# Sliding-window copy: which direct copies go whole and which in two halves

## The chip, the cores and the metric

The kernel runs on one core of a Trainium2 chip. The metric is device time in microseconds (us), the median of several runs. The kernel does no arithmetic: everything that takes time is a transfer by the core's 16 DMA engines.

## The reference

```
x: (32, 4096, 256) float32, window_size = 64, stride = 32
n_windows = (4096 - 64) // 32 + 1          # 127
for i in range(n_windows):
    result[:, i] = x[:, 32 * i : 32 * i + 64]
```

Call 32 rows of x (32 x 256 float32, 32 KB) a block. A batch of x has 128 blocks, and window i of a batch is block i followed by block i + 1. So nearly every block is written twice: as the first half of its own window and as the second half of the window before. The output is 266 MB, the input 134 MB.

## The kernel before

**Two ways for the data.** Batches 1, 4, 7, ..., 31 (11 of 32) are *staged*: `Staging.load` brings the 128 blocks of a batch (4 MB) into one of six SBUF tiles `xb`, one block to a partition, and `Staging.store` writes the tile out twice, once as first halves and once as second halves of windows (4 MB each). The other 21 batches go *directly* from DRAM to DRAM, by `Copier.windows`.

**The staging ring** is issued on ScalarE's DMA queue (`ring_s`, q10 in the profile): six loads, six items' stores, five loads, five items' stores. The descriptors are 16 KB, so a load or one half of an item's store gives each of the 16 engines 16 data packets and one semaphore packet: 17 packets. Of the first and last items some transfers are cut smaller. A store also writes one half-window that belongs to the neighbour batch, which is why the windows at the batch edges are written later.

**The direct copies** are issued on SyncE's DMA queue (`ring_d`, q1). `sixteens` lists 147 groups of 16 windows (1 MB of output each). A group goes in one of two forms:

- *whole*: one DMA of 16 rows of 64 KB; each engine gets two 32 KB packets and one semaphore packet, 3 packets ("turns" in the code);
- *halves*: one DMA with the 16 first halves and one with the 16 second halves, 512 KB each; each engine gets two times one 32 KB packet and one semaphore packet, 4 packets.

Both forms move the same bytes. The loop at L175 chooses by an accumulator, `share`, that grows per group; when it reaches 120, 120 is taken off and the group goes in halves. `turns` counts the packets that one engine has got from this queue, and the ring's own packets are taken to pass at the same count: `first_loads` = 102, then 204 for the stores, `loads` = 85. `loading` (L178) is true in the two loading stretches so counted. Neither the order of the groups nor anything on the ring's queue depends on the form chosen.

**The end.** The DMA before the last group's signals `near` (L176). GpSimd's queue (`ring_r`, q0) waits for it (L192) and then issues the 21 `edges`, up to 15 windows each (20.5 MB with the columns of L200), waiting for the store of each neighbouring staged item (L196). SyncE waits for the last item's first stores (L201) and then copies two last windows in columns (L202). The kernel ends when all counts are in (L204).

Of the kernel before, what the change touches and what calls it, by code (L numbers as in the profile page):

```python
# [125 lines left out]
@with_exitstack  # L126
def kernel(
    ctx: ExitStack,
    tc: tile.TileContext,
    x: bass.AP,  # L130
    window_size: bass.AP,
    stride: bass.AP,
    out: bass.AP,
):
    nc = tc.nc
    W, S = int(window_size), int(stride)
    B, L, D = x.shape
    n_win = (L - W) // S + 1
    assert out.shape == (B, n_win, W, D)
    c = Copier(x, out, B, L, D, W, S, n_win)  # L140


    staged = [*range(1, B, 3)]
    items = [(b, -1 if b == B - 1 else 0, c.nb) for b in staged]
    place = {b: g for g, (b, _, n) in enumerate(items) if n == c.nb}
    direct = [b for b in range(B) if b not in staged]
    pool = ctx.enter_context(tc.tile_pool(name="xb", bufs=1))
    st = Staging(c, tc, pool, x.dtype, items, 6)
    ring_d, ring_s, ring_r = nc.sync, nc.scalar, nc.gpsimd
    done = tc.alloc_semaphore("done")  # L150
    near = tc.alloc_semaphore("near")
    rest = tc.alloc_semaphore("rest")
    total = {done: 0, near: 0, rest: 0}

    def count(dma, sem):
        dma.then_inc(sem, 16)
        total[sem] += 16

    sixteens = []
    for b in direct:
        w = 15 if b - 1 in staged else 0
        sixteens += [(b, w + 16 * j) for j in range((c.nw - w) // 16)]
    singles = [(B - 1, c.nw - 1, 1)]
    edges = [(b, 0 if b - 1 in staged else 112, 15) for b in direct[:-1]]
    last = B - 2
    edges.append((last, 112, 4))

    first_loads, loads, stores = 6 * 17, 5 * 17, 6 * 34  # L170
    turns = share = 0
    with tc.tile_critical():  # L172
        st.run(ring_s)

        for i, (b, w) in enumerate(sixteens):  # L175
            sem = near if i == len(sixteens) - 2 else done  # L176
            second = turns - first_loads - stores
            loading = turns < first_loads or 0 <= second < loads  # L178
            share += 120 if turns < 16 or -8 <= second < 16 else 90 if loading else 18
            if share >= 120:  # L180
                share -= 120
                turns += 4
                count(c.windows(ring_d, b, w, 16, 0), done)
                count(c.windows(ring_d, b, w, 16, 1), sem)
            else:
                turns += 3
                count(c.windows(ring_d, b, w, 16), sem)
            if i == len(sixteens) // 2:
                for b, w, half in singles:
                    count(c.windows(ring_d, b, w, 1, half, 2048), done)  # L190

        ring_r.wait_ge(near, 16)  # L192
        for b, w, n in edges:
            for k in (b - 1, b + 1):
                if k in place and b != last:
                    st.wait_stored(ring_r, place[k])  # L196
            count(c.windows(ring_r, b, w, n), rest)


        count(c.columns(ring_r, last, 116, 9), rest)  # L200
        st.wait_stored(ring_d, place[B - 1])  # L201
        count(c.columns(ring_d, last, 125, 2), done)  # L202
        total[st.ended] = st.count[st.ended]
        for sem, n in total.items():  # L204
            ring_d.wait_ge(sem, n)
# [35 lines left out]
```

## Time and profile before

| | |
|---|---|
| time, median of 3 runs | 744.95 us (744.84 to 745.9) |
| span of the profiled execution | 749.4 us |
| profiled execution's own time | not recorded apart from its span |
| mean rate of the 16 DMA engines over the span | 418 GB/s |
| bytes moved by DMA | 313.26 MB in 18290 packets |
| GpSimd issues the first 18 edges | 654.4 to 664.7 us |
| the other 3 and the columns | 702.0 to 704.3 us |
| SyncE issues the last columns | 729.8 us, landing after 9.4 us |

A packet is one descriptor's worth of data on one DMA engine (here 16 KB or 32 KB, and a few bytes for a semaphore). The windows view of the profile gives, for each stretch, the busy time and count of the compute engines (here GpSimd alone, which only issues), the granted TensorE clock (no matter here), the DMA engines' mean busy share and the GB/s that they moved.

### The profile page before, as it was taken

The page shows a single profiled execution, that of the slowest core. Times are in us where ns is not written, and L with a number is a line of the kernel's source. Part 1 is how long each engine was busy: PE and PEld are TensorE (multiplying, and loading weights), DVE is VectorE, ACT ScalarE, POOL GpSimd, SP SyncE. Part 2 cuts the span into 40 slices and gives each one's busy share as a digit, 9 for nine tenths or more (in the row PEclk, how much of TensorE's full clock was granted, in tenths as well). Part 3 has the DMA queues.
Part 4 walks back from the last instruction along what each step waited for, and adds up shares of the span by engine and source line. Part 5 has one row for each costly group of instructions (what it writes and reads, how often), then busy time and mean ns, then how long its engine had stood idle before and what let it go on. Part 6 is the DMA issues. An engine that isn't in the chain of part 4 may idle for free.

```text
span 749.4 us, 322 instructions
## 1 busy us (share of the span) xinstructions
POOL 12.8 (2%) x26
## 2 busy tenths in 40 slices
POOL 0000000000000000000000000000000000040100
DMA  8999999999999999999999999999999999999996
GB/s 360 401 427 429 427 429 428 434 423 418 420 424 423 418 424 415 422 427 427 414 427 417 429 432 429 430 422 430 429 423 421 423 421 419 425 426 423 431 409 262
DMA packets 18290, 313.26 MB, mean 418 GB/s; under 512 B 4336, under 2 KB 4336, under 8 KB 4528
## 3 DMA queue, kind: packets, MB, share of 16 engines
q1 hardware_dynamic: 8016, 154.32, 48.8%
q10 hardware_dynamic: 9104, 138.41, 44.0%
q0 software_dynamic: 1168, 20.51, 6.5%
q14 instruction: 2, 0.02, 0.0%
HBM read 220.95 MB, written 267.09 MB: 651 GB/s over the span
## 4 chain that ended last, share of the span: by engine, by line
another core or an unknown queue 92%; POOL 2%; issue 0%; POOLq 0%; SPq 0%
POOL out_dram L34 2%; POOL out_dram L44 0%; POOLq L236 0%; SPq L172 0%; POOLq L114 0%
## 5 line engine op out<-in xcount | busy, mean ns | idle before, releaser
L34 POOL DMA_DIRECT2D out_dram<-in_x_dram x21 | 12.0, 576 | 691.3 <-DMA out_dram<-in_x_dram 654.0
L44 POOL DMA_DIRECT2D out_dram<-in_x_dram x1 | 0.6, 581 | 0.0
L222 POOL MEMSET const-float32-0.0<- 128x1 f32 x1 | 0.1, 98 | 0.2 <-issue 0.2
L222 POOL MEMSET const-bfloat16-1.0<- 128x1 bf16 x1 | 0.1, 101 | 0.0
L222 POOL MEMSET const-float32-1.0<- 128x1 f32 x1 | 0.1, 98 | 0.0
L222 POOL MEMSET const-uint8-127<- 128x1 uint8 x1 | 0.1, 98 | 0.0
## 6 DMA issues: line engine op xcount, KB each, us to landing
out_dram<-in_x_dram SPq DMA_DIRECT2D x92, 1024.0 KB, 100.7
out_dram<-xb ACTq DMA_DIRECT2D x21, 4096.0 KB, 139.7
out_dram<-in_x_dram SPq DMA_DIRECT2D x110, 512.0 KB, 90.3
xb<-in_x_dram ACTq DMA_DIRECT2D x10, 4096.0 KB, 131.4
out_dram<-in_x_dram POOLq DMA_DIRECT2D x20, 960.0 KB, 38.5
xb<-in_x_dram ACTq DMA_DIRECT2D x4, 1024.0 KB, 15.7
out_dram<-xb ACTq DMA_DIRECT2D x2, 1024.0 KB, 113.4
out_dram<-xb ACTq DMA_DIRECT2D x4, 512.0 KB, 96.9
```

Of the source, the lines that this page charges most:

```text
L34: return q.dma_start(out=self.oap((b * self.nw + w0) * 2 + h, [[2 * blk, n], row]), in_=self.xap(b * self.nb + w0 + h, [[blk, n], row]), m ...
L44: return q.dma_start(out=self.oap((b * self.nw + w0) * 2, [[part, 16], [2 * self.blk, n], row]), in_=self.xap(b * self.nb + w0, [[part, 16 ...
L222: nc = _bacc.Bacc("TRN2", target_bir_lowering=False, num_devices=1)
```

## The change

The step of `share` is replaced. Before, groups go in halves in the first 16 turns and from 8 turns before the second loads to 16 turns into them, three in four while the ring loads, and 18 in 120 while it stores. After, they go in halves in the first 16 turns, whole while the ring loads, and 82 in 120 while it stores.

```diff
             loading = turns < first_loads or 0 <= second < loads
-            share += 120 if turns < 16 or -8 <= second < 16 else 90 if loading else 18
+            share += 120 if turns < 16 else 0 if loading else 82
             if share >= 120:
```

Counted by running the loop, by the stretch in which `turns` stands when a group is issued:

| stretch | before: halves / whole | after: halves / whole |
|---|---|---|
| first loads | 21 / 6 | 4 / 29 |
| first stores | 11 / 54 | 38 / 18 |
| second loads | 18 / 4 | 0 / 28 |
| second stores | 5 / 28 | 20 / 10 |
| all | 55 / 92 (496 turns) | 62 / 85 (503 turns) |

The order within the stores is, after, halves, halves, whole, repeated, with three halves in a row now and then. The instructions of ScalarE's and GpSimd's queues are unchanged; SyncE's queue has seven instructions more.

## The prediction

> **What bounds the kernel now.** I read the page first. Three DMA queues carry everything, and together they fill the 16 engines' time.
>
> ```profile
> q1 hardware_dynamic: 8016, 154.32, 48.8%
> q10 hardware_dynamic: 9104, 138.41, 44.0%
> q0 software_dynamic: 1168, 20.51, 6.5%
> HBM read 220.95 MB, written 267.09 MB: 651 GB/s over the span
> ```
>
> The three shares make 99.3% of the span: the engines have no idle time to win back, and the change moves no byte (a group is 1 MB in either form). Time can only come from the pace of the packets, so next I cut the span into stages in the windows view. The cuts are where the ring's packet count (the DMA view of a window from 0: 1680 packets of q10 by 131.7 us, 105 per engine) shows loads turning into stores.
>
> ```profile
> 0.00:35.00 35.00, 0.20 (x4) 1.00 0.94 377
> 35.00:131.00 96.00, 0.00 (x0) 1.00 1.01 428
> 131.00:150.00 19.00, 0.00 (x0) 1.00 1.01 434
> 150.00:405.00 255.00, 0.00 (x0) 1.00 1.00 422
> 405.00:412.00 7.00, 0.00 (x0) 1.00 1.02 405
> 412.00:513.00 101.00, 0.00 (x0) 1.00 1.01 429
> 513.00:530.00 17.00, 0.00 (x0) 1.00 1.00 431
> 530.00:650.00 120.00, 0.00 (x0) 1.00 1.01 422
> ```
>
> The last column is GB/s. The loading stages, mostly halves, run at 428 and 429. The storing stages, mostly whole, run at 422, except for their first 17 to 19 us (434, 431). An undisturbed pace is about 431: the packet records have medians of 1213 ns for 32 KB, 611 ns for 16 KB and 9 ns for a semaphore, and a whole group beside three ring packets comes to 430 by these, a pair of halves beside four to 429, plus under 1% because packets overlap by some 4 ns. So form alone makes no pace: the loss is in packets that last longer than their median. Summed over the records it is 15.0 us per engine. Storing at 422 instead of 431 for 255 and 120 us is 7.8 us of it, loading 1.1 us; the rest is the start and the end.
>
> The two queues alternate packet by packet: by 654 us q1 had 7949 packets and q10 7954. That lets me place each group in time: its turn number times 16 is its place among q1's packets. Of the storing stages, three stretches of halves, two of halves where one store DMA ends and the next begins, and three of whole groups:
>
> ```profile
> 205.30:210.20 4.90, 0.00 (x0) 1.00 1.01 431
> 262.00:266.80 4.80, 0.00 (x0) 1.00 1.01 434
> 349.70:354.60 4.90, 0.00 (x0) 1.00 1.00 428
> 292.60:296.90 4.30, 0.00 (x0) 1.00 1.00 412
> 318.20:323.00 4.80, 0.00 (x0) 1.00 0.97 410
> 157.80:175.30 17.50, 0.00 (x0) 1.00 1.00 419
> 275.10:288.20 13.10, 0.00 (x0) 1.00 1.00 420
> 569.30:577.90 8.60, 0.00 (x0) 1.00 1.00 419
> ```
>
> And single whole groups amid the loads:
>
> ```profile
> 96.30:100.50 4.20, 0.00 (x0) 1.00 1.03 437
> 114.50:118.80 4.30, 0.00 (x0) 1.00 1.03 442
> 476.70:480.90 4.20, 0.00 (x0) 1.00 1.00 429
> ```
>
> In a storing stage halves run undisturbed in mid-store and slow at a store's end; whole groups are slow throughout. Amid loads a whole group is not slow. Windows this short carry packets over their edges, so I take prices from the records: the time above the median, as a share of all packet time while a group passes. Storing: 81 whole groups 2.30%, 14 pairs of halves 0.99% (the pair at 406 us, where stores turn into loads, apart: 10.3%). Loading, from 36 us on: 9 whole groups 0.60%, 33 pairs 0.77%.
>
> **Part by part. Storing.** A whole group takes 3 turns and about 4.2 us, a pair 4 turns and 4.86 us. Before, whole groups fill 82 x 4.2 = 344 us of the stores' 422 us, 81%; after, 28 x 4.2 = 118 us beside 58 x 4.86 = 282 us, 29%. So 52% of 400 us goes from 2.30% to 0.99%: 400 x 0.52 x 1.31% = 2.7 us won. Bounds: by the windows view alone (13 stretches of halves average 424.1 GB/s, the stage 422, so whole ones 421.5) the difference is 0.6% and the gain 1.3 us; if halves free the stores down to the loading stages' 0.74%, it is 2.16% less 0.74% of 400 us, 5.7 us. The row nearest to the changed code is the 14 pairs, so 2.7.
>
> **Loading.** 34 pairs fewer, 47 whole groups more; the stages last longer for the direct stream moves more per turn, but this is shifted work, not added work. From 36 us on some 230 us change form. By the nine whole groups the price is 0.60% less 0.77%, nothing; by the storing rows it would be 2.30% less 0.74%, 3.6 us lost. I take 0, because those nine ran in this very stage; but none of them ran beside another whole group, so the other bound stays in the range.
>
> **The start.** Up to 35 us the rate is 377. Turns under 16 stay halves, the fifth group stays whole (12.1% above the median at 22 to 26 us), but the sixth and seventh (8.7% and 1.5%, 5 us each) become whole. At the fifth's 12.1% that is 5 x 3.4% and 5 x 10.6%, 0.7 us lost; at the price of later whole groups it is a gain of 0.5. I take 0.3 lost, nearer to the loss since the fifth is their neighbour.
>
> **The turn into the second loads.** The halves laid around it go: at 405 to 412 us the rate was 405 in spite of them. Nothing in the trace shows what whole groups do there; at 2.3% instead of 10.3% they would win 0.4 us, at a doubled price lose 0.5. I take 0.
>
> **Semaphores and issue.** Seven more DMAs give each engine seven more 9 ns packets, 0.06 us. SyncE issues a DMA about 90 to 100 us ahead of its landing (the issue rows), so seven instructions more on its queue are hidden; if that lead were gone, each would cost about 0.57 us (the shortest issue), 4 us in all. Nothing else is moved past that queue.
>
> **The end.** The direct stream has 503 turns instead of 496, so `near` comes when the ring has passed 7 more packets per engine, 7 x 0.58 = 4.0 us later, less what the stores won. Who waits for it is GpSimd:
>
> ```profile
> POOL out_dram L34 <- DMA out_dram<-in_x_dram: 654.0, 1, 654.0
> ```
>
> That wait ends at some 656 us instead of 654.0. After it q0 has 73 packets per engine (1168 / 16) and the ring 569 - 503 = 66 left instead of 73. In the last seven turns q0 has no partner, but these are the 4 KB packets of the columns (159 ns each, 1.1 us in sum), counted already. The wait for the ninth item's store (37.4 us before) ends while q0 still has edges queued, as before. I cost the end at 0; if q0 alone can't fill the engines, it costs up to 2 us.
>
> **Sum.** -2.7 + 0 + 0.3 + 0 + 0.06 + 0 = -2.3 us. The profile records no time of its own beside the span of 749.4 us, which lies 4.5 us above the median of the runs; I take the difference from the median: 744.95 - 2.3 = 742.6 us.
>
> **Two rules of the skill.** The Trainium skill's DMA: Bandwidth & Descriptors, section Bandwidth, speaks against the change: it wants at least 1 MiB per DMA, and its section on the anatomy of a DMA puts about 2 us of fixed cost on each. With that, seven more DMAs would make the sum an estimated 14 us worse if nothing overlapped. The trace disagrees: a 512 KB DMA behind others ends in a 9 ns packet, and pairs in mid-store ran at 428 to 434. The HBM Reference, section Specifications, gives 716 GB/s for the memory domain; whole groups draw an estimated 1.59 x 430 = 682 beside loads and beside stores alike, so by that page neither stage should slow, and the storing rows do.
>
> **The rivals.** *Nothing moves* (744.9, within 0.7): the slow packets belong to the stores, wherever a store DMA ends, and the 14 pairs were cheap by where they happened to stand. For it: pairs at a store's end ran at 410 and 412. Against it: the mid-store pairs at 428 to 434 beside whole groups at 419 and 420.
>
> *Slower* (746.6): a run of whole groups beside loads is as slow as one beside stores. Mechanism: a whole group puts 59% of the bytes on the path that both reads and writes DRAM, and the memory, not the engines, sets the pace. Place: 36 us to the end of the first loads, and the second loads; price 3.6 us, with 0.7 at the start; less 2.7 is +1.6. For it: every whole group amid loads stood alone, and in both storing stages it took 17 us of whole groups before the rate fell. Against it: 0.60% on those nine. It decides once the loading stages lose 2.4 us over about 230 us, 1.0%, which is a rate under 424 there.
>
> *More than forecast* (739.8): the stores fall to the loading stages' share, 5.7 us won, 0.5 lost elsewhere. For it: pairs that follow pairs may be freer than the lone ones seen. Against it: the ends of the stores.
>
> That the change does not do what it says I can exclude: the loop's own count gives the table of forms.
>
> **How the numbers follow.** Forecast 0.40, nothing 0.22, slower 0.28, more 0.10. A difference of 0.2%, 1.5 us, is about what a measurement of this kernel can tell from no change. The forecast lies 0.3% below; with its bounds some of it falls within 0.2%, and so does the near side of the slower case. Faster by over 0.2%: 0.47; within: 0.25; slower: 0.28. The range goes from 739.6 (a large gain) to 747.2 (the slower case, with the end or the turn into the loads 0.8 us worse). The forecast's own range is 740.8 to 744.2.
>
> **What would show it.** Right: the stages in which the ring stores at 425 GB/s or more with dips only at the ends of store DMAs, loading stages at 428 or more, `near` at about 656 us, the last packet some 2 us earlier. Wrong: storing stages still at 422; loading stages at 424 or less; or a rate below 400 between the ring's end and the last column packet.

## The result: slower by 0.6%

The changed kernel takes 749.18 us (median of 4 runs, 748.62 to 752.38), the kernel before 745.42 us beside it. The ratio over the runs is 1.0064, with a 95% interval of 1.0050 to 1.0078; the two medians by themselves are 3.76 us, 0.5%, apart. The forecast was 742.6 us and its range ended at 747.2: the sign was wrong.

The windows view of the changed kernel, cut at its own stages (columns as before: stretch, its length, GpSimd's busy time and count, clock, DMA share, GB/s):

```profile
35.00:148.00 113.00, 0.00 (x0) 1.00 1.01 415
150.00:395.00 245.00, 0.00 (x0) 1.00 1.01 432
400.00:520.00 120.00, 0.00 (x0) 1.00 1.01 415
525.00:655.00 130.00, 0.00 (x0) 1.00 1.01 432
660.00:700.00 40.00, 11.54 (x21) 1.00 1.01 433
720.00:740.00 20.00, 0.00 (x0) 1.00 1.00 381
```

The two stages have changed places. Storing went from 422 to 432, the undisturbed pace; loading went from 428 and 429 to 415. And from 720 to 740 us, where the ring has little left and the edges are 5.55 of the 7.62 MB moved, the rate is 381 (408 in the first profile of the kernel before). The wait that releases the edges moved too:

```profile
POOL out_dram L34 <- DMA out_dram<-in_x_dram: 658.5, 1, 658.5
```

It was 654.0 before and forecast at 656. In two executions of more typical length (below) it goes from 648.8 to 655.3: 6.5 us later, of which the seven turns explain an estimated 4.0 and the stages, as it turns out, about the rest. The second wait, for the ninth item's store, became shorter (25.5 us instead of 37.4): the edges come to it 4.6 us later, and it ends 7.3 us earlier.

In all that follows, *slow time* is what I summed from the packet records: for each packet its duration less the median for its size (1213 ns for 32 KB, 611 for 16 KB, 159 for 4 KB, 9 for a semaphore), divided by 16 for the time per engine. Without it every kernel that does the whole work needs the same engine time, 729.6 us give or take 0.5. A stage begins and ends here where the ring's packet count passes from loads to stores or back; the start is the first 35 us, and the end begins with the first packet of the edges.

### The profile page after: what moved, and what is told of

Same layout as the page of the kernel before. It is cut to its first block, busy times and chain, and to the rows that moved or that the text cites. A ratio compares the mean times of both kernels' runs of the same rounds, so it can differ in the third digit from the quotient of the medians.

```text
span 750.6 us, 329 instructions
## 1 busy us (share of the span) xinstructions
POOL 12.7 (2%) x26
## 2 busy tenths in 40 slices
DMA packets 18402, 313.26 MB, mean 417 GB/s; under 512 B 4448, under 2 KB 4448, under 8 KB 4640
## 3 DMA queue, kind: packets, MB, share of 16 engines
HBM read 220.95 MB, written 267.09 MB: 650 GB/s over the span
## 4 chain that ended last, share of the span: by engine, by line
another core or an unknown queue 91%; POOL 2%; issue 0%; POOLq 0%; SPq 0%
POOL out_dram L34 2%; POOL out_dram L44 0%; POOLq L236 0%; SPq L172 0%; POOLq L114 0%
```

## Experiments

### Second profiles of both kernels

> The kernel before, unchanged, for a second profile. Its first profile has a span of 749.4 us beside runs of 745; in the later runs a kernel's time is its span and 1.8 us, so that execution took some 751 us and is 6 us longer than its kernel. If that execution was a bad sample of the storing stretches (2.3 and 1.9% above the median there), a second one with a span near 743 shows 1% or less in them, 3 to 5 us per engine instead of 9. If it was a fair sample, the storing stretches show about 2% again.

> The changed kernel, unchanged, for a second profile; its first (752.4 us) lies 3.2 us over the median of its other runs. Loading stretches 3 to 4% above the median and storing stretches clean again if these are the change's doing; in a fair sample the sum of the slow packets is 10 to 12 us per engine and the last packets come 3 us earlier.

The executions took 745.12 and 748.86 us (spans 743.3 and 747.1). Kernel before, then changed kernel, same windows:

```profile
35.00:130.00 95.00, 0.00 (x0) 1.00 1.01 431
155.00:395.00 240.00, 0.00 (x0) 1.00 1.00 427
410.00:505.00 95.00, 0.00 (x0) 1.00 1.01 432
530.00:650.00 120.00, 0.76 (x2) 1.00 1.00 427
```

```profile
35.00:130.00 95.00, 0.00 (x0) 1.00 1.01 419
155.00:395.00 240.00, 0.00 (x0) 1.00 1.01 432
410.00:505.00 95.00, 0.00 (x0) 1.00 1.00 418
530.00:650.00 120.00, 0.00 (x0) 1.00 1.01 432
```

The kernel before stores at 427 in an execution of typical length, not at 422: the profile that the prediction was worked from came from an execution some 6 us longer than the kernel's runs, and showed 9.1 us of slow time in the storing stages where this one shows 4.0. The difference of the two typical executions closes: loading 0.7 to 7.6 us (+6.9), storing 4.0 to 0.2 (-3.8), start 1.4 to 1.5, end 1.6 to 2.3 (+0.7), in sum +3.9; the times differ by 3.74 us. The changed kernel's first profile was long too (752.4 us, where its other runs took 748.6 to 749.4): it has 9.3 us of slow time in the loading stages, so the 415 GB/s above are lower than the 418 and 419 of a typical execution.

Slow time in us per engine, one profiled execution of each kernel (the numbers behind the readings below; *its time* is that execution's, which also varies with how long some engines stand idle at the very end, on average 2.3 to 5.3 us of the last 20 by the packet records):

| kernel | pairs | start | loading | storing | end | sum | its time |
|---|---|---|---|---|---|---|---|
| before, first profile | 55 | 2.2 | 1.5 | 9.1 | 2.2 | 15.0 | span 749.4 |
| before, again | 55 | 1.4 | 0.7 | 4.0 | 1.6 | 7.7 | 745.1 |
| changed, first profile | 62 | 1.6 | 9.3 | 0.2 | 3.0 | 14.1 | 752.4 |
| changed, again | 62 | 1.5 | 7.6 | 0.2 | 2.3 | 11.6 | 748.9 |
| storing half alone | 106 | 1.4 | 1.5 | 0.9 | 12.7 | 16.6 | 753.2 |
| loading half alone | 16 | 1.6 | 8.0 | 4.0 | 1.7 | 15.3 | 750.9 |
| fewer pairs | 55 | 1.7 | 7.6 | 0.8 | 1.5 | 11.5 | 747.4 |
| uniform | 55 | 1.3 | 4.2 | 0.7 | 1.2 | 7.4 | 744.0 |
| uniform, no pairs | 4 | 1.5 | 4.1 | 2.0 | 1.1 | 8.8 | 745.0 |
| between | 55 | 1.3 | 1.9 | 2.2 | 1.7 | 7.1 | 746.1 |
| 60 and 42 in 120 | 61 | 1.5 | 3.1 | 1.0 | 2.3 | 7.9 | 744.5 |
| the same, edges earlier | 61 | 1.7 | 2.5 | 0.9 | 2.0 | 7.1 | 743.0 |

### Each half of the change alone

Here and below the edits are shown against the changed kernel, in the loop at L175; unchanged lines are left out.

```diff
-            share += 120 if turns < 16 else 0 if loading else 82
+            share += 120 if turns < 16 or -8 <= second < 16 else 90 if loading else 82
```

> The storing half of the change alone: groups go in halves at 82 in 120 while the ring stores, and while it loads they keep the step of before (90 in 120, and the pairs at the turn). 106 pairs, 547 turns on the direct queue instead of 496 (before) and 503 (after). Theory 'stretches': the time per packet is set by how the direct groups are cut in each stretch, loading and storing apart, so both stretches run at 428 GB/s or more, slow packets in them come to under 2 us per engine (13 us before), and what is lost is only the end: the direct queue now outlives the ring by some 50 turns, with the edges alone on the engines at 10 to 15% above the median, 5 to 7 us. Time 742 to 746. Rival 'end': the end decides more than the stretches do; the 51 turns more cost in proportion to the change's own 3.8 us for 7 turns, over 10 us, so 750 or more.

Measured: 754.09 us (753.17 to 755.03), ratio 1.0117 (1.0103 to 1.0130). Both theories have a part: the stretches are clean as the first said (430 and 431 GB/s in all four), and the end costs as much as the second said, twice what I had priced. The edges begin at 679 us with about 2 MB left in the ring, and from 704 us on nothing else runs:

```profile
680.00:700.00 20.00, 7.02 (x13) 1.00 1.02 376
705.00:725.00 20.00, 0.00 (x0) 1.00 1.00 333
725.00:735.00 10.00, 0.00 (x0) 1.00 1.05 344
```

Direct copies by themselves go at some 335 GB/s, not 430. What 51 more pairs won in the stretches, 2.3 us of slow time, they lost several times over here, 11.1 us.

```diff
-            share += 120 if turns < 16 else 0 if loading else 82
+            share += 120 if turns < 16 else 0 if loading else 18
```

> The loading half of the change alone: whole groups while the ring loads, 18 in 120 while it stores as before. 16 pairs, 457 turns. 'Stretches': loading stretches at 413 to 417 GB/s as in the changed kernel, storing stretches at 422 as before, about 7 us more slow packets than before; the ring outlives the direct copies, which costs little as its packets are even over the engines. Time 750 to 754. 'End': the direct queue is done 39 turns early, so the edges never run alone and the time is that of before or less, 742 to 746, in spite of the loading stretches.

Measured: 752.79 us (750.62 to 756.94), ratio 1.0104 (1.0080 to 1.0127). Loading at 417 and 415 GB/s, storing at 427 as before (this kernel also lacks the pairs laid around the turn into the second loads): here the stretches decide, and a short direct queue doesn't save the kernel. The two halves alone lose 9.0 and 7.7 us; together they lose 3.8, because the pairs that one puts in are taken out by the other and the end stays near its place.

### The end alone

```diff
-            share += 120 if turns < 16 else 0 if loading else 82
+            share += 120 if turns < 16 else 0 if loading else 72
```

> The changed kernel with 72 instead of 82 in 120 while the ring stores: 55 pairs and 496 turns, so that the direct queue and the edges end with the ring as before. 'Stretches' with the end's 7 turns as a part of the loss: storing stretches still at 428 or more, loading stretches at 413 to 417, the end with slow packets like before; time 2 us below the changed kernel, 746 to 748. 'Loading alone': the end's length makes no difference, 749.

Measured: 747.65 us (747.08 to 749.3), ratio 1.0034 (1.0021 to 1.0046): 1.5 us under the changed kernel. The end's slow time goes from 2.3 to 1.5 us, to that of before; storing rises to 0.8, loading stays at 7.6; the rest of the 1.5 us lies in how evenly the engines finish (idle at the very end 3.5 us in the one profile, 2.3 in the other), which differs from execution to execution. So seven turns at the end cost about 1 us, and with the end as before 2.5 us are still lost. By slow time it would be 3.7, the loading stages' 6.9 less the 3.2 that storing won; in the profiled execution less idle time at the very end makes up the difference.

### Is it the form or the proportion?

```diff
-            share += 120 if turns < 16 else 0 if loading else 82
+            share += 120 if turns < 16 else 43
```

> One step for both stretches, 43 in 120 (55 pairs, 496 turns as before; halves in the first 16 turns). 'Stretches', with a threshold: a mixture in between keeps the direct copies' share of the bytes (about 0.555) under what slows the packets in the storing stretches (0.535 ran clean, 0.575 lost 2%) or lies just at it: storing stretches 426 or more, loading stretches 421 to 426, time 742 to 745. Without a threshold, each stretch in proportion to its whole groups: the losses add up to those of before, 745 to 747. 'End': 496 turns, so the time of before, 745.4.

Measured: 744.78 us (744.03 to 746.13), ratio 0.9997 (0.9988 to 1.0006). No difference in time, but the stretches are not those of before, as the first loads and the first stores show:

```profile
35.00:130.00 95.00, 0.00 (x0) 1.00 1.00 422
155.00:395.00 240.00, 0.00 (x0) 1.00 1.00 431
```

Storing has 0.7 us of slow time with only every third group in halves, loading 4.2. So a whole group in the storing stages has no fixed price of its own; above some proportion of them the slow packets begin.

```diff
-            share += 120 if turns < 16 else 43
-            if share >= 120:
-                share -= 120
+            share += 240 if turns < 16 else 43
+            if turns < 16:
+                share -= 240
...
+            elif share >= 240:
+                share -= 240
+                turns += 5
+                count(c.windows(ring_d, b, w, 16, None, DIRECT // 2), sem)
```

> The uniform mixture with another form: beyond the first 16 turns no group goes in halves; 25 groups go whole but in 16 KB packets (four and a semaphore to each engine, 5 turns), half as many as there were pairs, so that the turns stay at 495 and the direct copies' share of the bytes at 0.555. If the share decides ('stretches'), time and stretches are those of the uniform mixture: 744 to 746, loading about 2%, storing about 0.2% above the median. If the form decides, that is, if whole groups are what disturbs (rows of 64 KB side by side, each block read twice within one DMA), loading stretches go to 3.5% and storing ones to 1 to 2%, and the time to 750 or more.

Measured: 745.39 us (743.84 to 746.68), ratio 1.0003 (0.9992 to 1.0013). Loading 4.1 us as in the uniform mixture; storing 2.0 us, 0.5%, between the 0.2% of the one expectation and the 1 to 2% of the other, perhaps since five turns at a time mix more coarsely (not tested). Time and loading stages follow the proportion. A kernel with no pairs beyond the first 16 turns runs as fast as the kernel before.

> Direct groups alone: the staged batches, the edges and the columns are left out; 72 groups in halves, a wait for them, then 75 whole. If the path that reads and writes DRAM has a ceiling of its own, whatever the form, both parts run equally slow, at 350 to 380 GB/s instead of 430 (in the stores-only kernel the edges alone ran 19% above the median at the end), each part some 200 us. If halves are easier on DRAM, their part runs at 400 or more and the whole ones' at 370 or less.

The whole run took 469.6 us. Three rows of its windows, halves in the first two and whole groups in the third:

```profile
10.00:100.00 90.00, 0.00 (x0) 1.00 1.00 332
100.00:200.00 100.00, 0.00 (x0) 1.00 1.00 336
300.00:400.00 100.00, 0.00 (x0) 1.00 1.00 334
```

Equal: the ceiling has nothing to do with the form. A byte of these is read from DRAM and written to it (the profile counts 154.14 MB read and 154.14 MB written), so 334 GB/s is 668 GB/s of DRAM traffic, and the median 32 KB packet takes 1540 ns instead of 1213.

The same count for the stages leads to the cause. The DMA view of a window lists what each queue moved; q1's bytes cross DRAM twice, the ring's once. The kernel before (35 to 130 us, then 155 to 395), then the changed kernel, same windows; columns are packets, MB, share of the engines' time:

```profile
q1 hardware_dynamic: 1236, 21.96, 53.9%
q10 hardware_dynamic: 1224, 19.01, 47.1%
```

```profile
q1 hardware_dynamic: 2838, 58.43, 57.3%
q10 hardware_dynamic: 2844, 43.98, 43.1%
```

```profile
q1 hardware_dynamic: 1064, 23.33, 57.7%
q10 hardware_dynamic: 1068, 16.45, 42.8%
```

```profile
q1 hardware_dynamic: 3127, 55.12, 53.5%
q10 hardware_dynamic: 3132, 48.43, 47.1%
```

| | direct share of bytes | GB/s | DRAM traffic, GB/s |
|---|---|---|---|
| before, loading | 0.54 | 431 | (2 x 21.96 + 19.01) / 95 us = 662 |
| before, storing | 0.57 | 427 | (2 x 58.43 + 43.98) / 240 us = 670 |
| changed, loading | 0.59 | 419 | (2 x 23.33 + 16.45) / 95 us = 664 |
| changed, storing | 0.53 | 432 | (2 x 55.12 + 48.43) / 240 us = 661 |

The engines' own pace of 431 needs 1.59 x 431 = 685 GB/s at the changed kernel's loading share, and gets 664: 3% missing, which is the 419. At its storing share it needs 661 and gets it. The two rows that fall short of the engines' pace stop at 664 and 670, and the direct copies alone at 668; the other two need no more than the 661 and 662 that they get. That is what a ceiling on the DRAM traffic would do, at nearly the same height whether direct copies are 0.57, 0.59 or all of the bytes; which part of the path to DRAM sets it, no run shows. The kernel before sits just under the ceiling while loading and at it while storing. Over the whole kernel the profile's 220.95 + 267.09 MB at 668 GB/s make 731 us, and its 313.26 MB at 431 make 727: two bounds, half a per cent apart.

### Mixtures in between

```diff
-            share += 120 if turns < 16 else 0 if loading else 82
+            share += 120 if turns < 16 else 60 if loading else 34
```

> Between the kernel before and the uniform mixture: 60 in 120 while the ring loads, 34 in 120 while it stores, halves in the first 16 turns; 55 pairs, 496 turns. Theory 'ceiling': beside loads the direct copies and the ring together get no more than about 658 GB/s of DRAM traffic, beside stores about 670, whatever the form, so what one stretch gains the other gives back: loading stretches 2.5 to 3 us of slow packets (0.7 before, 4.2 uniform), storing ones 1 to 2 us (4.0 before, 0.7 uniform), time 744 to 745, at most 0.1% below the kernel before. Rival 'threshold': both stretches fall under what slows them, slow packets under 2 us together, time 741 to 743.

Measured: 744.45 us (743.28 to 746.75), ratio 0.9989 (0.9977 to 1.0000), as the ceiling theory expected; the slow time is 1.9 us in loading (it said 2.5 to 3) and 2.2 in storing (1 to 2), twice what its rival allowed in sum.

Two more, with 60 in 120 while the ring loads and 42 while it stores, and in the second the edges released two groups earlier:

```diff
-            share += 120 if turns < 16 else 60 if loading else 34
+            share += 120 if turns < 16 else 60 if loading else 42
...
-            sem = near if i == len(sixteens) - 2 else done
+            sem = near if i == len(sixteens) - 4 else done      # second kernel only
```

> 60 in 120 while the ring loads, 42 in 120 while it stores: 61 pairs, 502 turns, nearly the turns of the changed kernel with the pairs spread over both stretches. Theory 'ceiling': loading 2 us and storing 0.7 us of slow packets (4.0 and 0.7 in other mixtures), the end 0.5 to 0.8 us worse than before for six turns more; time 743 to 744.3. Rival: the end's six turns cost as much as they free, 745 to 746.

> As the run above, with the edges released two groups earlier, so that they start some 6 turns sooner and end with the ring. If the end's loss is that the edges outlive the ring, this wins 0.5 to 0.8 us over the run above, 742.5 to 743.8; if three queues at once put the direct copies' share above the ceiling for as long, the two are equal.

Measured: 744.46 us (ratio 0.9999, 0.9986 to 1.0012) and 744.59 us (0.9994, 0.9985 to 1.0003). The slow time is 3.1 and 2.5 us in loading and about 1 in storing, with an end of 2.3 and 2.0 us: what the stretches win, the end takes, and the earlier release wins nothing that shows. The first kernel's time lies between its two expectations, and its loading stages lost more than the 2 us expected. None of the mixtures beats the kernel before by more than its measurement can tell.

## Why the prediction was wrong, step by step

- **The bound** was read right, but only half: the engines are full, and the pace of their packets decides. A second bound, DRAM traffic, lies within 1% of it; I named it as the slower rival's mechanism, weighed it at 0.28 and left it out of the sum.
- **Storing**: forecast -2.7 us, measured -3.8. The sign held, and the size came near by luck. I took a price per whole group (2.30% against 0.99%) from an execution 6 us too long; the same count over the second profile gives about 1.2% against 0.2%, which would have made some 2 us. In fact neither form has a price of its own. At a share of 0.53 the stage falls below the ceiling and the whole groups in it are free too, so nearly all of the stage's loss went, whatever it was (9.1 us in one profile, 4.0 in the other).
- **Loading** is the step that failed: forecast 0, with 3.6 us as the other bound, measured +6.9. The nine whole groups amid loads stood alone in a stage whose share was 0.54, so their 0.60% says nothing of a stage made of whole groups, whose share is 0.59: that stage asks for 685 GB/s of traffic and gets 664. The rival's own price was also too low, since it borrowed the storing stages' 2.30%, which belongs to a share of 0.57. The rival's sign, mechanism and place are what the runs show.
- **The start**: forecast +0.3, measured +0.1. **The turn into the second loads** is contained in the loading and storing rows, and no run measured it by itself. **Semaphores and issue**: as forecast, the seven semaphores cost 0.06 us of engine time, and nothing shows a cost of the issue.
- **The end**: forecast 0, with up to 2 us if the engines could not be filled; measured 0.7 us in the second profiles, and about 1 us by the run with fewer pairs. The engines are filled, but more and more with direct copies, which by themselves run at 335 GB/s.
- **The sum against the median**: I took a difference made in a 749.4 us execution as valid for a 745 us kernel. Of the 7.3 us more of slow time in it, 5.1 were in the stage that the change was to relieve.
- **Two slips in the numbers**: the loading stages have 35 pairs fewer, not 34 (39 against 4 in the table of forms), and the slower rival with 0.8 us more ends at 747.4, not 747.2; neither changes the outcome. And the whole groups' rows at 419 and 420 were the low ones: others in the storing stages ran at up to 428.
- **The skill's rules**: that a DMA wants 1 MiB (the Trainium skill, DMA: Bandwidth & Descriptors, section Bandwidth, where it is measured on loads into SBUF issued from GpSimd) had no part in it: 512 KB halves and 1 MB whole groups alone ran at 336 and 334. The 716 GB/s of the HBM Reference (section Specifications) was not reached: where traffic limits, the rows above stop at 664 to 670, so the estimate of 682 that looked safe by that page was over the measured ceiling.

What stays open: why the loading stages already lose time at a share of 0.56 (4.2 us in the uniform mixture) where the storing ones hardly do (0.7). The ceiling seems to lie 1% lower when the traffic is mostly reads (660 and 664 GB/s in the uniform mixture's two loading stretches, 670 in its first storing one); no run took reads and writes apart. In the changed kernel's first loads the ring's 16 KB packets lasted on average 35 ns over their median (6%), the 32 KB direct ones 16 ns (1%).

A plain ceiling also doesn't say why slow packets gather. In the second profile of the kernel before, about two thirds of the slow time in the first stores falls into the quarter of each store DMA's time that lies around its end, as the *nothing moves* rival had it; in the changed kernel the same ends cost nothing (0.2 us in all). So the ends of the stores matter only where the share is high, and why they do is not shown.

## What to carry to other kernels

When the DMA engines are full, count the DRAM traffic too, with a copy inside DRAM at twice its bytes: here both bounds lie within 1%. What counts is that no stage asks for much more than the ceiling, not that one stage runs free: shares of 0.59 and 0.53 lost 3.8 us, while 0.54 and 0.57, or 0.56 throughout, took the same time. A slow packet is then a matter of the mixture around it, so a price per copy read from isolated ones can't be carried to a run of them. And set the profiled execution's length against the runs' before any stage's loss is taken from it.

## What the hardware showed that I had not expected

Copies from DRAM to DRAM alone go at 334 GB/s (668 GB/s of traffic) on 16 engines that move 431 when half of the bytes come from or go to SBUF. The onset is sharp: beside stores, a demand of 661 GB/s left 0.2 us of slow time in all, one of about 677 (1.57 x 431) 4.0 us. With nothing beside them, whether a megabyte went as one DMA or two made no difference (334 and 336 GB/s).
